# A hybrid attention and DeltaNet block on one core: one place for the matmuls' operands in memory, a tile of its own for turned q, k, v, and an earlier place for the output's first loads

## The chip, the core and the metric

The kernel runs on one core of a Trainium2 chip. The metric is device time in microseconds (us), as the median of runs; lower is better. Five instruction streams matter: PE (TensorE, matmuls and transposes), DVE (VectorE), ACT (ScalarE), POOL (GpSimd) and SP (SyncE, which here only issues DMAs). Each stream runs its instructions in the order in which they were written. PEld in a profile is the loading of a matmul's stationary operand.

## What is computed

One decoder block on x of 1024 tokens by 1024 features, fp32, from the reference, cut:

```python
h = rmsnorm(x, norm1_w)
proj = h @ w_in            # sb_q, sb_k, sb_v, sb_z, g_q, g_k, g_v, g_z, g_b, g_a
o_sb = stick_breaking_attention(sb_q, sb_k, sb_v)        # 8 heads of 64
o_sb = rmsnorm(o_sb, sb_norm_w) * silu(sb_z)
qkv = silu(causal_depthwise_conv([g_q, g_k, g_v], gdn_conv_w))   # 4 taps
o_gdn = gated_delta_chunked(l2norm(gq), l2norm(gk), gv, decay, beta)  # 4 heads of 128
o_gdn = rmsnorm(o_gdn, gdn_norm_w) * silu(g_z)
x = x + concat([o_sb, o_gdn]) @ w_out
return rmsnorm(x, final_norm_w)
```

## The kernel before

**Matmuls in three parts.** Nearly all large products run on numbers of type fp32r: an operand is split into a high part `h` (a copy rounded to fp32r by ACT) and a low part `l` (the remainder, by DVE or POOL), and `mm3` makes h·h, h·l and l·h. In a matmul the moving operand streams past (usually 512 columns) and the stationary one (128 x 128) is loaded ahead of it. In a profile's names `pp<-xl,weh` the tile ahead of the arrow is the PSUM bank; in the product of input and weights `xh`, `xl` (input) move and `weh`, `wel` (weights) are stationary.

**Stages.** First q for the attention (`wqh`, `wql`), then v and the DeltaNet's gates from the weights `chl` (eight tiles of 2 x 520 columns, in h and l: 264 columns for the first half of v, 256 for the second). Then `projections()` goes through the other columns in the fixed order ORDER, while the attention (`window`, tiles `kh`, `kl`, `q`, `ahl`, `v2a`) and the DeltaNet (`gdn_pre`, `gdn_inv`, `gdn_chain`) run between its matmuls. At the end come the output's products: first the DeltaNet's half (`products_delta`, eight blocks of 128 tokens, weights `wo`), then the attention's (`products_attention`, weights `woh`, `wol`). In these the weights move and the block's values `mmf` are stationary.

**What sets the order.** The kernel is written as streams that yield; a small planner (`Model`, `interleave`) replays them with costs of its own and fixes the order of the instructions on every engine and of the DMAs on SP. The third argument of a `Stream` is the rank of its instructions: of those that are ready the lowest goes first. Any change of a tile, a wait or a rank therefore moves instructions all over the program.

**Names that the text uses.** `g_evac` (lines 901 to 938) takes the projection of a DeltaNet q, k or v: ACT copies it into `pre` (two buffers, pool gd), DVE and ACT form the convolution in PSUM and `ac`, ACT writes the sigmoid into the same `pre`, POOL multiplies `ac` by it. For heads 2 and 3 DVE then turns `ac` in squares of 32 by 32, and four DMAs store it:

```python
sg = pre[:, 0:512]
...
first(V.transpose, sg, ac)
turned = gt_s[h, kind, ts, :].rearrange("(b r) d -> r b d", r=32)
done += [S.dma_start(turned[:, :, 32 * a:32 * a + 32], sg[32 * a:32 * a + 32, :]...) for a in range(4)]
```

So `pre` is free again only when those DMAs have read it. `k_evac` and `z_evac` use a one-buffer tile tagged `sqh` for the high part of k and for the gate's sigmoid `zs`.

`enter_delta` (line 1553) loads, for each block of the DeltaNet's half, its values (`mgf<-og_s`) and its gate (`mgf<-gate_s`); `split` multiplies them (DVE), and ACT and POOL make the parts `mmf`. `out_norm` (line 1452) loads the attention's finished outputs (`bothf<-o_s`, four DMAs a block), which ACT, DVE and POOL (`oss`) normalise for the second half.

**Places in memory.** Each tile has an address within the partition. By the program as built, taken modulo 256 bytes, moving and stationary operand of the fp32r matmuls stand so:

| matmuls (moving, stationary) | number | before: moving, stationary |
|---|---|---|
| projections `xh`/`xl`, `weh`/`wel` | 1152 | 96, 96 |
| q `xh`/`xl`, `wqh`/`wql` | 192 | 96, 96 |
| scores `kh`/`kl`, `q` | 192 | 160, 160 |
| attention's values `ahl`, `v2a` | 160 | 160, 0 or 224 |
| v and gates `chl`, `xh`/`xl` | 384 | 0 to 224, 96 |
| output, DeltaNet's half `wo`, `mmf` | 192 | 0, 32, 96, 160 or 224, 128 |
| output, attention's half `woh`/`wol`, `mmf` | 204 | 64, 128 |

So 1,576 of these have both operands at one place modulo 256, and 900 have not.

Of the kernel before, what the change touches and what calls it, by code (L numbers as in the profile page):

```python
# [10 lines left out]
F32 = mybir.dt.float32  # L11
# [6 lines left out]
P = 128  # L18
T = 1024
# [472 lines left out]
def block(tc, xT_d, x_d, n1_d, wE_d, wQ_d, wC_d, conv_d, alog_d, dtb_d, mixw_d, wo_d, fnw_d, out_d):  # L492
# [4 lines left out]
    with ExitStack() as top:  # L497
# [66 lines left out]
        xl = px.tile([P, NK, T], F32R, name="xl")  # L564
        s0_ctx = top.enter_context(ExitStack())
        s0 = open_pool("s0", ctx=s0_ctx)
        n1 = s0.tile([P, 24], F32, name="n1")[:, 0:NK]
        rbc = s0.tile([P, T], F32, name="rbc")

        def turned(tp, parts):  # L570
# [45 lines left out]
        def q_evac(pt, i, half):  # L616
            hs = slice(half * 512, (half + 1) * 512)
            j = 2 * i + half
            apart = j == 3
            if apart:  # L620
                hi, lo = [pr.tile([P, 512], F32R, tag="kt", bufs=2, name="xq") for _ in range(2)]
            else:
                t = at_.tile([P, 2, 512], F32R, tag="ahl", bufs=2, name="xq") if j in (1, 5) else s0.tile([P, 2, 512], F32R, tag="xr", bufs=5, name="xq")
# [12 lines left out]
        chl = []  # L636
        for tag, bufs in (("kh", 1), ("kl", 1), ("q2", 1), ("v2a", 1), ("sg2", 1), ("cc", 2), ("cc", 2), ("sg3", 1)):
            if tag[0] == "s":
                chl.append(fx.tile([P, 2, 520], F32R, "chl", tag))
            elif tag == "v2a":  # L640
                chl.append(Two(*[at_.tile([P, 520], F32R, tag=tag + c, name="chl") for c in "xy"]))
            else:
                t = at_.tile([P, 1040 + (48 if tag == "kl" else 0)], F32R, tag=tag, bufs=bufs, name="chl")
                chl.append(t[:, 0:1040].rearrange("p (a e) -> p a e", a=2))
# [70 lines left out]
        for b in range(NB):  # L715
            wc = s0.tile([P, 520], F32, tag="wcr", bufs=6, name="wcr")
            loads[f"c{b}"] = [S.dma_start(wc, wC_d[:, b, :])]
            A.activation(chl[b][:, 0, :], wc, AF.Copy)
            (V if b < 2 else G).tensor_tensor(chl[b][:, 1, :], wc, chl[b][:, 0, :].bitcast(F32), ALU.subtract)
        loads["s"] = [scale]  # L720
        first_loads = [op for name in LOADS for op in loads[name]]
        for a, b in zip(first_loads, first_loads[1:]):
# [39 lines left out]
        for k0 in range(0, NK, 2):  # L762
            for b in range(NB):
                bs = slice(b * P, (b + 1) * P)
                for k in (k0, k0 + 1):
                    mm3(vp[b][:, 0:264], xh[:, k, bs], xl[:, k, bs], chl[k][:, 0, 0:264], chl[k][:, 1, 0:264], k == 0, k == NK - 1)
# [30 lines left out]
        def values():  # L797
            for b in range(NB):
                yield lambda: ps.room("pp", 2)
                bs = slice(b * P, (b + 1) * P)  # L800
                pt = pp()
                for k in range(NK):
                    mm3(pt[:, 0:256], xh[:, k, bs], xl[:, k, bs], chl[k][:, 0, 264:520], chl[k][:, 1, 264:520], k == 0, k == NK - 1)
# [97 lines left out]
        def g_evac(h, kind):  # L901
            wv = conv[:, 4 * kind + h, :]
            last = []

            def evac(pt, half):
                pre = gd.tile([P, 515], F32, tag="pre", bufs=2, name="pre")
                if half == 0:
                    A.activation(pre[:, 0:3], step[:, 0:3], AF.Copy)
                else:
                    A.activation(pre[:, 0:3], last[0][:, 512:515], AF.Copy)  # L910
                last.append(pre)
                first(A.activation, pre[:, 3:515], pt, AF.Copy)
                ac = pr.tile([P, 512], F32, tag="kt", bufs=2, name="ac")

                first(A.activation, pt, pre[:, 0:512], AF.Copy, scale=wv[:, 0:1])
                for i in range(1, 4):
                    first(V.scalar_tensor_tensor, ac if i == 3 else pt, pre[:, i:i + 512], wv[:, i:i + 1], pt, ALU.mult, ALU.add)
                sg = pre[:, 0:512]
                first(A.activation, sg, ac, AF.Sigmoid)
                ts = slice(half * 512, half * 512 + 512)  # L920
                if h < TURNED and kind < 2:
                    kq = operand(h, half)
                    ck.prio, prio = BANK, ck.prio
                    r = G.tensor_tensor(kq[:, :, 1 - kind, :], ac.rearrange("p (c t) -> p c t", c=4), sg.rearrange("p (c t) -> p c t", c=4), ALU.mult)
                    ck.prio = prio
                    return r
                first(G.tensor_tensor, ac, ac, sg, ALU.mult)
                if h < TURNED:
                    return S.dma_start(g_s[h, kind, :, ts], ac)
                ck.prio, prio = STORES, ck.prio  # L930
                done = [S.dma_start(g_s[h, kind, :, ts], ac)] if kind < 2 else []
                first(V.transpose, sg, ac)
                turned = gt_s[h, kind, ts, :].rearrange("(b r) d -> r b d", r=32)
                done += [S.dma_start(turned[:, :, 32 * a:32 * a + 32], sg[32 * a:32 * a + 32, :].rearrange("r (b c) -> r b c", c=32)) for a in range(4)]
                ck.prio = prio
                return done

            return evac
# [387 lines left out]
        def attention():  # L1326
            yield lambda: "v1" in flags and "dec" in flags
            for i in range(2):
                ccs.append(at_.tile([P, T + 1], F32, tag="cc", bufs=2, name="cc"))
# [169 lines left out]
            ck.free(w)  # L1499

        def out_weights():
            places = [(t, 2 if t in ("cc", "ahl") else 1) for t in ("kh", "kl", "q2", "cc", "cc", "v2a", "ahl", "ahl")]
            for n, k in enumerate(range(4, 8)):
                yield lambda: k in raws and (n < 2 or f"e{SBH - 1}3" in flags)
                yield raws[k][1]
                weight(k, *[Two(*[at_.tile([P, 512], F32R, tag=t + c, name="wo") for c in "xy"]) if t == "v2a" else at_.tile([P, D], F32R, tag=t, bufs=m, name="wo") for t, m in places[2 * n:2 * n + 2]])
                yield

        def out_weights_attention():
            yield lambda: "g" in flags  # L1510
            gdn_ctx.close()
            f0 = pools[0] = open_pool("f0", before=gd.ops())
            flags["pool0"] = True
            for k in range(4):
                yield lambda: k in raws
# [114 lines left out]
        def products_attention():  # L1630
            yield lambda: f"d{NB - 1}" in flags
            for b in range(NB):
# [3 lines left out]
                for got in product(b, 0, parts):  # L1636
# [87 lines left out]
```

## Time and profile before

| what | value |
|---|---|
| median of 3 runs | 637.1 us (636.01 to 638.25) |
| the profiled execution | 638.77 us, its span 637.0 us |
| busy: PE, DVE, ACT, POOL | 98%, 71%, 62%, 54% of the span |
| mean granted PE clock | 0.993 |
| DMA moved | 115.99 MB, mean 182 GB/s |

The span runs from the first to the last instruction; 1.77 us of the profiled execution lie around it. The busy share of PE counts each matmul from its start to a modelled end, and successive matmuls overlap, so time that is lost between matmuls is read from their starts.

### The profile page before, as it was taken

To read this page: it belongs to the slowest core of one execution; us is meant where nothing else is said; L and a number is where in the kernel's file an instruction comes from. 1 tells how busy PE (TensorE), PEld (TensorE's weight loads), DVE (VectorE), ACT (ScalarE), POOL (GpSimd) and SP (SyncE) were. 2 spreads that over 40 slices of the span, in tenths; PEclk is the share of its full clock that TensorE was granted. 3 is DMA by queue.
4 is the path that set the end of the run, shared out by engine and by line. 5 is a ranking of instruction groups with operands and counts; after the bars stand their busy time and mean duration, and the time that the engine had idled before them with its cause. 6 is when DMAs were issued, how large, how long until landed. Compare 5 with 4: busy or idle time off the path is not lost.

```text
span 637.0 us, 11159 instructions
## 1 busy us (share of the span) xinstructions
PE 623.7 (98%) x3672; PEld 528.3 (83%) x3672; DVE 451.4 (71%) x799; ACT 396.1 (62%) x957; POOL 345.7 (54%) x429
## 2 busy tenths in 40 slices
PE   8999999999999999899999999999999998999995
PEld 7889988988888888788888888888878886887884
DVE  4469974322787896796789687677898875387774
ACT  5765578724786784776688766576868753132553
POOL 0124047828795596692697682486753426145533
PEclk9999999999999999999999999999999998999998
DMA  8968326866317428678747974525562387987642
GB/s 301 330 204 309 118 87 205 269 195 216 105 40 259 135 78 227 161 183 220 216 109 157 298 206 139 188 92 152 154 190 67 133 179 263 291 243 167 159 136 99
DMA packets 162233, 115.99 MB, mean 182 GB/s; under 512 B 95168, under 2 KB 130176, under 8 KB 162176
## 3 DMA queue, kind: packets, MB, share of 16 engines
q1 hardware_dynamic: 161888, 115.09, 60.4%
q8 instruction: 29, 0.48, 0.3%
q14 instruction: 28, 0.23, 0.1%
q10 hardware_dynamic: 288, 0.20, 0.1%
HBM read 78.12 MB, written 37.13 MB: 181 GB/s over the span
## 4 chain that ended last, share of the span: by engine, by line
PE 83%; issue 4%; DMA 4%; POOL 3%; DVE 2%; ACT 2%; SPq 1%; POOLq 0%; DVEq 0%; ACTq 0%
PE pp L376 49%; PE pz L376 23%; PE po L376 7%; PE pc L376 3%; POOL mmf L376 1%; DMA dtf<-cum_s 1%; SPq L376 1%; DMA gate_s<-zt 1%; DMA gt_s<-pre 1%; DVE cc L376 1%; DMA mgf<-og_s 0%; POOL dtf L376 0%; POOL oss L376 0%; DMA og_s<-akf 0%; DVE pp L376 0%
## 5 line engine op out<-in xcount | busy, mean ns | idle before, releaser
L376 PE MATMUL pp<-xh,weh 128*128 128x512 f32 x360 | 145.7, 405 | 0.0
L376 PE MATMUL pp<-xh,wel 128*128 128x512 f32 x360 | 141.3, 392 | 0.0
L376 PE MATMUL pp<-xl,weh 128*128 128x512 f32 x360 | 140.6, 390 | 0.0
L376 POOL TENSOR_TENSOR sgf<-sgf,cc 128x128 f32<-128x128 f32 (+3 forms) x64 | 77.1, 1208 | 48.8 <-DVE cc L376 45.1
L376 POOL TENSOR_TENSOR wel<-wer,weh 128x512 fp32r<-128x512 f32 x48 | 63.1, 1316 | 67.4 <-ACT weh L376 67.4
L376 PEld LDWEIGHTS pp<-xh,wel 128*128 128x128 f32 x360 | 67.5, 188 | 15.2
L376 PEld LDWEIGHTS pp<-xh,weh 128*128 128x128 f32 x360 | 67.7, 188 | 11.9
L376 PEld LDWEIGHTS pp<-xl,weh 128*128 128x128 f32 x360 | 67.8, 188 | 11.6
L376 DVE TENSOR_TENSOR_SCAN cc<-pz,step 128x384 f32<-128x384 f32 (+2 forms) x64 | 53.9, 847 | 8.1 <-ACT pz L376 6.7
L376 ACT ACTIVATE sgf<-pz,rs 128x384 f32<-128x384 f32 (+3 forms) x96 | 54.2, 593 | 7.4 <-PE pz L376 7.3
L376 ACT ACTIVATE ahl<-pz 128x512 fp32r<-128x512 f32 (+1 forms) x80 | 43.5, 559 | 19.9 <-PE pz L376 19.1
L376 DVE TENSOR_TENSOR ahl<-pz,ahl 128x512 fp32r<-128x512 f32 (+1 forms) x80 | 49.3, 628 | 6.5 <-ACT ahl L376 6.2
L376 ACT ACTIVATE pz<-pz,ns 128x384 f32<-128x384 f32 (+3 forms) x96 | 53.5, 575 | 0.0
L376 PE MATMUL po<-ahl,v2a 128*128 128x512 f32 (+1 forms) x160 | 49.1, 400 | 1.1 <-DVE ahl L376 1.1
L376 PE MATMUL pp<-wo,mmf 128*128 128x512 f32 x192 | 47.7, 407 | 2.2 <-POOL mmf L376 1.4
L376 PEld LDWEIGHTS pp<-wo,mmf 128*128 128x128 f32 x192 | 36.7, 194 | 12.0 <-POOL mmf L376 1.8
L376 DVE SCALAR_TENSOR_TENSOR pp<-pre,conv,pp 128x512 f32<-128x512 f32 x42 | 31.4, 747 | 20.2 <-ACT pp L376 19.7
L376 PE MATMUL pp<-woh,mmf 128*128 128x512 f32 (+2 forms) x136 | 41.8, 384 | 0.0
L376 DVE TENSOR_TENSOR_SCAN cc<-pz,cc,step 128x512 f32<-128x512 f32 (+1 forms) x32 | 38.7, 1208 | 3.6 <-ACT pz L376 3.1
L376 DVE TENSOR_TENSOR xr<-pp,xr 128x512 f32<-128x512 f32 (+2 forms) x33 | 22.1, 672 | 23.7 <-PE pp L376 23.4
L376 POOL TENSOR_TENSOR mmf<-mgf,mmf 128x512 fp32r<-128x512 f32 x16 | 21.8, 1375 | 29.0 <-ACT mmf L376 29.0
L376 PE MATMUL pz<-kh,q 128*128 128x384 f32 (+3 forms) x96 | 35.7, 377 | 0.9 <-DVE cc L376 0.9
(318 smaller groups left out, 1522.5 us busy)
## 6 DMA issues: line engine op xcount, KB each, us to landing
wer<-wE SPq DMA_DIRECT2D x48, 256.0 KB, 4.0
xr<-x SPq DMA_DIRECT2D x16, 512.0 KB, 7.0
v_s<-v2e SPq DMA_DIRECT2D x16, 256.0 KB, 2.7
v2a<-v_s SPq DMA_DIRECT2D x16, 256.0 KB, 2.9
q<-qk_s SPq DMA_DIRECT2D x8, 512.0 KB, 4.0
kh<-qk_s SPq DMA_DIRECT2D x8, 512.0 KB, 3.7
kl<-qk_s SPq DMA_DIRECT2D x8, 512.0 KB, 7.2
o_s<-oe SPq DMA_DIRECT2D x32, 128.0 KB, 3.2
```

The lines of the kernel that those rows point to most:

```text
L376: ins = f(*args, **kw).ins
```

## The change

Three things. First, tiles are resized, padded and split, so that the operands of the fp32r matmuls stand at 128 modulo 256. In the table above, all rows but one become 128, 128. In the row of `chl` the 192 matmuls of 256 columns become 128, 128, and of the 192 of 264 columns 64 do; in all 2,348 pairs are equal and 128 are not. For this each weight tile `chl` is split in two (`c1` with 264 columns, `c2` with 256), so its high part takes two ACT instructions in place of one, and its low part two of DVE or POOL. Second, the turned q, k, v go to a tile `tn` that shares the one buffer tagged `sqh`. Third, `enter_delta` gets rank OUTPUT - 4 = 8 in place of 12; `out_norm` stays at 11. The diff, cut:

```diff
-        n1 = s0.tile([P, 24], F32, name="n1")[:, 0:NK]
+        n1 = s0.tile([P, 32], F32, name="n1")[:, 0:NK]
...
-        chl = []
-        for tag, bufs in (("kh", 1), ("kl", 1), ("q2", 1), ("v2a", 1), ("sg2", 1), ("cc", 2), ("cc", 2), ("sg3", 1)):
...
+        c1, c2 = [], []
+        for tag, size, n in (("kh", 1024, 2), ("kl", 1088, 2), ("q2", 1024, 2), ("v2ax", 512, 1), ("v2ay", 512, 1), ("cc0", 1088, 2)):
+            t = at_.tile([P, size], F32R, tag=tag, name="chl")
+            width = 264 if tag == "kl" else 256
+            (c1 if tag == "kl" else c2).extend(t[:, 2 * width * m:2 * width * (m + 1)].rearrange("p (a e) -> p a e", a=2) for m in range(n))
...
-            A.activation(chl[b][:, 0, :], wc, AF.Copy)
-            (V if b < 2 else G).tensor_tensor(chl[b][:, 1, :], wc, chl[b][:, 0, :].bitcast(F32), ALU.subtract)
+            for t, w in ((c1[b], wc[:, 0:264]), (c2[b], wc[:, 264:520])):
+                A.activation(t[:, 0, :], w, AF.Copy)
+                (V if b < 2 else G).tensor_tensor(t[:, 1, :], w, t[:, 0, :].bitcast(F32), ALU.subtract)
...
                 done = [S.dma_start(g_s[h, kind, :, ts], ac)] if kind < 2 else []
+                sg = pr.tile([P, 512], F32, tag="sqh", bufs=1, name="tn")
                 first(V.transpose, sg, ac)
...
-                kh = at_.tile([P, 1040], F32R, tag="kh", name="kh")[:, 16:1040]
+                kh = at_.tile([P, T], F32R, tag="kh", name="kh")
...
+            f0.tile([P, 16], F32, name="pad")
...
-                    Stream(enter_delta(), 9.3, OUTPUT), Stream(prepare(1), 9.2, OUTPUT), Stream(products_delta(), 101, OUTPUT),
+                    Stream(enter_delta(), 9.3, OUTPUT - 4), Stream(prepare(1), 9.2, OUTPUT), Stream(products_delta(), 101, OUTPUT),
```

The matmuls and their shapes are the same ones; ACT has 8 instructions more, POOL 6 and DVE 2.

What the ranks move is seen on SP, where the output's first loads are issued (`worf` are raw output weights, `og_s<-akf` stores the DeltaNet's results). Before:

```order
L376 DMA og_s<-akf_4143 32x16x32 x4
L376 DMA worf_6457<-wo 128x1024
L376 DMA bothf_6488<-o_s 32x32x32
L376 DMA o_s<-oe 128x256
L376 DMA bothf_6488<-o_s 32x32x32 x3
L376 DMA bothf_6493<-o_s 32x32x32 x4
L376 DMA mgf_6379<-og_s 128x512
L376 DMA mgf_6379<-gate_s 128x4x128
L376 DMA mgf_6382<-og_s 128x512
```

After:

```order
L376 DMA bothf_6466<-o_s 32x32x32
L376 DMA o_s<-oe 128x256
L376 DMA bothf_6466<-o_s 32x32x32
L376 DMA mgf_6360<-og_s 128x512
L376 DMA mgf_6360<-gate_s 128x4x128
L376 DMA mgf_6363<-og_s 128x512
L376 DMA mgf_6363<-gate_s 128x4x128
L376 DMA mgf_6421<-og_s 128x512
L376 DMA mgf_6421<-gate_s 128x4x128
L376 DMA bothf_6466<-o_s 32x32x32 x2
L376 DMA bothf_6471<-o_s 32x32x32 x4
```

Six of the eight loads `bothf` now stand behind the first six loads `mgf` in place of ahead of them. On ACT, at the start of the DeltaNet's products, before:

```order
L376 ACTIVATE bothf_6488<-bothf_6488 128x8x64
L376 ACTIVATE vr<-pc,r2b 128x128
L376 ACTIVATE kqf_4572<-pz 128x128
L376 ACTIVATE pz,norms<-pz 128x128
L376 ACTIVATE bothf_6493<-bothf_6493 128x8x64
L376 ACTIVATE kqf_4572<-pz 128x128
L376 ACTIVATE pz,norms<-pz 128x128
L376 ACTIVATE mmf_6625<-mgf_6379 128x512
```

After:

```order
L376 ACTIVATE mmf_6575<-mgf_6360 128x512
L376 ACTIVATE kqf_4657<-pz 128x128
L376 ACTIVATE pz,norms<-pz 128x128
L376 ACTIVATE mmf_6600<-mgf_6363 128x512
L376 ACTIVATE mmf_6618<-mgf_6421 128x512
L376 ACTIVATE zs<-pp 128x512
L376 ACTIVATE bothf_6466<-bothf_6466 128x8x64
L376 ACTIVATE bothf_6471<-bothf_6471 128x8x64
```

The first parts `mmf` now precede both blocks `bothf` and the last step of the DeltaNet's chain (`kqf`, `norms`). On SP, where the second and third turned tiles of head 2 are stored, before:

```order
L376 DMA g_s<-ac 128x512
L376 DMA gt_s<-pre 32x16x32
L376 DMA xd_101<-xs 32x16x16 x2
L376 DMA xe<-xs 64x128
L376 DMA gt_s<-pre 32x16x32 x2
L376 DMA akf_2913<-gt_s 128x4x128
L376 DMA gt_s<-pre 32x16x32
```

After, at the same place:

```order
L376 DMA g_s<-ac 128x512
L376 DMA gt_s<-tn 32x16x32 x4
L376 DMA kh<-qk_s 128x1x1024
L376 DMA q_2852<-qk_s 128x1x1024
L376 DMA kl<-qk_s 128x1x1024
L376 DMA o_s<-oe 128x256
L376 DMA g_s<-ac 128x512
L376 DMA gt_s<-tn 32x16x32 x4
```

The four stores of a turned tile now stand together, with other transfers between one tile and the next.

More of the change, by code (lines that the diff above doesn't have):

```diff
@@ L622, in q_evac @@
             else:
-                t = at_.tile([P, 2, 512], F32R, tag="ahl", bufs=2, name="xq") if j in (1, 5) else s0.tile([P, 2, 512], F32R, tag="xr", bufs=5, name="xq")
+                t = xq1 if j == 1 else at_.tile([P, 2, 512], F32R, tag="ahl", bufs=2, name="xq") if j == 5 else s0.tile([P, 2, 512], F32R, tag="xr", bufs=5, name="xq")
                 hi, lo = t[:, 0, :], t[:, 1, :]
@@ L633, in q_evac @@
             ck.prio = prio
-        chl = []
-        for tag, bufs in (("kh", 1), ("kl", 1), ("q2", 1), ("v2a", 1), ("sg2", 1), ("cc", 2), ("cc", 2), ("sg3", 1)):
[L638 to L644, printed above, removed]
+        c1, c2 = [], []
[3 more added lines that the diff above has]
+            (c1 if tag == "kl" else c2).extend(t[:, 2 * width * m:2 * width * (m + 1)].rearrange("p (a e) -> p a e", a=2) for m in range(n))
+        for tag, n in (("sg2", 2), ("sg3", 3)):
+            t = fx.tile([P, 528 * n], F32R, "chl", tag)
+            c1.extend(t[:, 528 * m:528 * (m + 1)].rearrange("p (a e) -> p a e", a=2) for m in range(n))
+        xq1 = at_.tile([P, 2, 512], F32R, tag="ahl", bufs=2, name="xq")
+        c1.append(at_.tile([P, 528], F32R, tag="cc1", name="chl").rearrange("p (a e) -> p a e", a=2))
         sm = fx.tile([P, 768], F32, "sm", "sg1")
@@ L765, in block @@
                 for k in (k0, k0 + 1):
-                    mm3(vp[b][:, 0:264], xh[:, k, bs], xl[:, k, bs], chl[k][:, 0, 0:264], chl[k][:, 1, 0:264], k == 0, k == NK - 1)
+                    mm3(vp[b][:, 0:264], xh[:, k, bs], xl[:, k, bs], c1[k][:, 0, :], c1[k][:, 1, :], k == 0, k == NK - 1)
             for k in (k0, k0 + 1):
@@ L802, in values @@
                 for k in range(NK):
-                    mm3(pt[:, 0:256], xh[:, k, bs], xl[:, k, bs], chl[k][:, 0, 264:520], chl[k][:, 1, 264:520], k == 0, k == NK - 1)
+                    mm3(pt[:, 0:256], xh[:, k, bs], xl[:, k, bs], c2[k][:, 0, :], c2[k][:, 1, :], k == 0, k == NK - 1)
                     if k % 2 and k < NK - 1:
@@ L1328, in attention @@
             for i in range(2):
-                ccs.append(at_.tile([P, T + 1], F32, tag="cc", bufs=2, name="cc"))
+                ccs.append(at_.tile([P, T + 1], F32, tag=f"cc{i}", name="cc"))
                 V.memset(ccs[i][:, T:T + 1], 0.0)
@@ L1501, in out_weights @@
         def out_weights():
-            places = [(t, 2 if t in ("cc", "ahl") else 1) for t in ("kh", "kl", "q2", "cc", "cc", "v2a", "ahl", "ahl")]
+            places = [(t, 2 if t == "ahl" else 1) for t in ("kh", "kl", "q2", "cc0", "cc1", "v2a", "ahl", "ahl")]
             for n, k in enumerate(range(4, 8)):
```

## The prediction

> **What bounds the kernel now.** I read the page's busy times first, then the chain that ended last, then who PE waited for.
>
> ```profile
> span 637.0 us, 11159 instructions
> PE 623.7 (98%) x3672; PEld 528.3 (83%) x3672; DVE 451.4 (71%) x799; ACT 396.1 (62%) x957; POOL 345.7 (54%) x429
> PE 83%; issue 4%; DMA 4%; POOL 3%; DVE 2%; ACT 2%; SPq 1%; POOLq 0%; DVEq 0%; ACTq 0%
> ```
>
> PE is busy for 98% of the span and makes up 83% of the chain; no other engine comes near. So a matmul that starts the next one sooner is worth what it saves, almost anywhere, and work of another engine counts only where PE stands still for it. PE's waits (engine, for whom: us in total, times, longest) are few:
>
> ```profile
> PE pp L376 <- POOL mmf L376: 1.4, 1, 1.4
> PE po L376 <- DVE ahl L376: 1.1, 1, 1.1
> PE pz L376 <- DVE cc L376: 0.9, 1, 0.9
> PE pp L376 <- ACT mmf L376: 0.8, 2, 0.5
> ```
>
> The change speaks to all four: the lines with `mmf` lie at the output's first products, the other two, as shown below, behind a store of a turned tile. The rest of its bet is on the pace of the matmuls themselves.
>
> **First part: the operands' places.** The durations in the page overlap, so I take the pace from rows that merge many matmuls: start, us, how many. The first four are pieces of the chain, the other two of PE's timeline.
>
> ```profile
> 73.29 5.46 PE pp L376 x24
> 78.75 5.44 PE pz L376 x24
> 592.98 13.36 PE pp L376 x57
> 606.99 12.66 PE pp L376 x54
> 547.66 18.55 PE L376 MATMUL pp<-wo,mmf 128*128 128x512 f32 x79
> 277.19 1.89 PE L376 MATMUL pz<-kqf 128*128 128x256 f32 x8
> ```
>
> The projections, with both operands at 96, start one 512-column matmul every 5.46 / 24 = 227 ns. The output's second half, moving at 64 and stationary at 128, needs 13.36 / 57 = 234 ns; its first half, with mixed places, (18.55 - 0.39) / 78 = 233 ns, where 0.39 is the length of a single one. All have the same structure (three matmuls a pair of operands, nothing waited for), so of what I can see only the places differ. The groups that the change brings to equal places, and two that are equal already, by shape (count | busy us, mean ns of one | idle):
>
> ```profile
> L376 PE MATMUL pp<-xl,weh 128*128 128x512 f32 x360 | 140.6, 390 | 0.0
> L376 PE MATMUL pz<-kl,q 128*128 128x512 f32 x40 | 15.8, 394 | 0.0
> L376 PE MATMUL pp<-wo,mmf 128*128 128x512 f32 x192 | 47.7, 407 | 2.2 <-POOL mmf L376 1.4 <-ACT mmf L376 0.8
> L376 PE MATMUL pp<-woh,mmf 128*128 128x512 f32 x120 | 38.7, 397 | 0.0
> L376 PE MATMUL pp<-wol,mmf 128*128 128x512 f32 x60 | 23.7, 394 | 0.0
> L376 PE MATMUL po<-ahl,v2a 128*128 128x512 f32 x128 | 45.3, 430 | 1.1 <-DVE ahl L376 1.1
> L376 PE MATMUL pp<-chl,xh 128*128 128x256 f32 x96 | 18.2, 286 | 0.3 <-DVE v2e L376 0.3
> ```
>
> If equal places give 227 ns: `wo` 192 x 6 ns = 1.1 us, `woh` and `wol` 180 x 7 ns = 1.3 us, `ahl` 128 x 6 ns = 0.8 us. For `chl`, twice narrower, I take 2 ns for each of the 144 of 256 columns, 0.3 us. Together 3.5 us, all on PE's path. No row shows a 512-column matmul with both operands at 128. The ends are: 0, if the places have nothing to do with it, and 25 us. That end goes by the nearest row at 128, 128: the eight passes of `kqf`, (1.89 - 0.38) / 7 = 216 ns each (fp32, 256 columns, twice as long a column). If every 512-column fp32r matmul came to 216, the 1,424 with equal places would save 11 ns each (16 us) and the 500 others 17.5 ns (9 us). I take 3.5, since the equal pairs at 96 are the nearest in type and shape; that 128 is a better place than 96 nothing here shows.
>
> The Trainium skill, page "SBUF — State Buffer", section "Who interferes with whom", speaks against this term: PE has two independent read ports, one for the moving operand and one for the weights, and "PE and ACT never wait on anyone". By it the term is 0 and the sum 3.5 us higher, as in rival B below. The trace's 227 against 234 ns does not fit that page, unless something else in the output's stage slows PE. The page "TensorE: Matmul & The Clock Gate", section "Back-to-back issue gap", gives 512 / 2.4 + 2.5 = 216 ns, an estimate by which the projections' 227 have 11 ns to lose; whether their place is the cause it doesn't say.
>
> **Second part: the output's first loads.** PE's timeline, then SP, DVE, ACT and POOL at the start of the DeltaNet's products, then that stretch in a view by windows (clock after the busy times):
>
> ```profile
> 532.51 0.40 PE L376 MATMUL pp<-xh,wel 128*128 128x512 f32 x1
> 533.38 0.72 PE L376 MATMUL pp<-wo,mmf 128*128 128x512 f32 x2 [0.47 <-ACT mmf L376]
> 535.52 5.79 PE L376 MATMUL pp<-wo,mmf 128*128 128x512 f32 x17 [1.42 <-POOL mmf L376]
> 518.91 5.12 SPq L376 DMA_DIRECT2D bothf<-o_s  x7
> 524.08 0.76 SPq L376 DMA_DIRECT2D mgf<-og_s  x1
> 529.86 0.69 DVE L376 TENSOR_TENSOR mgf<-mgf 128x512 f32<-128x512 f32 x1
> 532.71 0.62 ACT L376 ACTIVATE mmf<-mgf 128x512 fp32r<-128x512 f32 x1
> 534.20 1.27 POOL L376 TENSOR_TENSOR mmf<-mgf,mmf 128x512 fp32r<-128x512 f32 x1
> 535.00:540.00 5.00, 4.48 (x13) 3.52 (x14) 1.27 (x2) 0.00 (x0) 5.00 (x5) 0.66 0.84 299
> ```
>
> PE's projections are over and it stands waiting for `mmf`: 533.38 - 532.51 - 0.23 = 0.64 us for ACT's part, then 535.52 - 533.38 - 2 x 0.233 - 0.1 = 1.58 us for POOL's (0.1 is how far the second row's two starts lie beyond the pace: 0.72 - 0.39 = 0.33 us between them). The clock answers: in the stretch of 5 us behind it is 0.66, and the 17 matmuls take (5.79 - 0.39) / 16 = 0.338 us each in place of 0.233, 16 x 0.105 = 1.68 us. Together 3.9 us. The reason is in the order: `mgf` is loaded only at 524.08, directly behind seven loads `bothf` of 5.12 / 7 = 0.73 us each, and DVE, ACT and POOL follow one another. In the changed order six loads `bothf` stand behind six `mgf`, so the first `mgf` is issued 6 x 0.73 = 4.4 us sooner (ends: 0 and 5.1), more than the 2.2 us that PE stood; ACT and POOL, whose queues had `bothf` and the DeltaNet's last step ahead, take `mmf` first. So I take the whole 3.9. The gain lies between 0 (the products wait for DVE or the last `og_s` instead) and 3.9. Below nothing it can go through what is late next: the attention's blocks `bothf` come six transfers, some 4.4 us, later (rival E), and the DeltaNet's last `kqf` stands on ACT behind an `mmf` of 0.62 us, which delays only the blocks that come last.
>
> **Third part: the tile `tn`.** The chain, ACT's, PE's and DVE's timeline, and DVE's group:
>
> ```profile
> 250.40 4.81 DMA gt_s<-pre
> 255.29 0.20 ACT L376 ACTIVATE pre<-pre 128x3 f32<-128x3 f32 x1 [5.28 <-DMA gt_s<-pre]
> 258.04 0.62 PE L376 MATMUL po<-ahl,v2a 128*128 128x512 f32 x2 [1.11 <-DVE ahl L376]
> 260.68 0.39 PE L376 MATMUL pz<-kh,q 128*128 128x256 f32 x1 [0.91 <-DVE cc L376]
> 248.35 0.71 DVE L376 STREAM_TRANSPOSE pre<-ac 128x512 f32<-128x512 f32 x1 [0.32 <-POOL ac L376]
> L376 DVE STREAM_TRANSPOSE pre<-ac 128x512 f32<-128x512 f32 x12 | 8.4, 704 | 2.4 <-POOL ac L376 1.6 <-DMA wer<-wE 0.7
> ```
>
> ACT stands 5.28 us for a store that reads `pre`, and just behind it PE stands for DVE's `ahl` and `cc`, which need ACT's results: 1.11 + 0.91 = 2.02 us by the rows. With `tn` ACT's next `pre` no longer needs that store, so those 2.0 us go, unless DVE is late there anyway. It is the only such wait that PE felt: the other tiles of the twelve cost it nothing. Against it: `tn` has one buffer, shared with `k_evac` and `z_evac`, where turned tiles had two. DVE's next transpose, or ACT's `zs`, must now wait for all four stores of the tile before. At this place the next transpose (248.35) would have stood until 250.40 + 4.81 = 255.2, 6.9 us. But the planner knows the wait and puts the four stores of a tile together, and DVE has 29% of its time free. Ends: -2.0 us, and +2.0 for each transpose that stands as long as ACT did. I take -2.0 (rival D is the other end).
>
> **Fourth part: more instructions, another order.** ACT's parts of `chl`, POOL's last work on them, and PE's chain at the last two weight tiles:
>
> ```profile
> L376 ACT ACTIVATE chl<-wcr 128x520 fp32r<-128x520 f32 x6 | 3.7, 639 | 0.2 <-DMA wcr<-wC 0.2
> 54.87 2.29 POOL L376 TENSOR_TENSOR chlf<-wcr,chlf 128x520 fp32r<-128x520 f32 x1
> 67.46 1.46 PE pp L376 x12
> ```
>
> Two halves for one of 0.639 us cost an instruction's fixed part more; the shortest ACT row here is 0.20 us (255.29), so 8 x 0.20 = 1.6 us on ACT, and as much on POOL and DVE. The last low part is ready at 54.87 + 2.29 = 57.2, PE takes the last weights at 67.46: 10 us of cover. I take 0 (ends 0 and 1.6). If that cover is gone, PE waits for the tile then at the head, at most those 1.6 us.
>
> And every instruction between is placed anew by the planner. PE's order changes all over, and a stall like the ones above can come up or go anywhere. The four rows of waits bound it: none of them costs PE over 2.2 us. I take +1.5, most of one such stall; ends 0 and two of 2.2.
>
> **Sum.** -3.5 - 3.9 - 2.0 + 0 + 1.5 = -7.9 us against the profiled execution of 638.8, which lies 1.7 above the median of 637.1. On the median: 629.2, said as 629 us. About 0.3%, 1.9 us, is what a measurement of this kernel can tell from no change.
>
> **The rivals.**
> B: the places do nothing. For it speaks that in the output's half other things than places differ too (weights move, DMAs run); against it that `woh`, with nothing waited for, stays at 234 over 57 matmuls in a row. 629.2 + 3.5 = 632.7.
> C: 128 is a better place than 96. For it speaks `kqf` at 216 ns; against it that `kqf` is fp32, whose columns take twice as long to stream, and that `kl,q` (both at 160) has the mean of the projections (394 and 390), so that the common place seems not to matter. Between 227 and 216 ns a matmul: 629 - 21 = 608 to 624.
> E: the places do nothing and the gain at 533 is given back at the attention's half. The chain there:
>
> ```profile
> 572.36 2.62 POOL oss L376
> 577.05 3.71 PE pp L376 x15
> ```
>
> POOL's `oss` stands in the chain just ahead of PE's next products, so `out_norm` has little slack at 577; `bothf` comes 4.4 us later, and PE would stand as long as it did at 533. It decides if DVE, ACT and POOL cannot make up those 4.4 us in the 40 us between. 632.7 + 3.9 = 636.6, no change.
> D, slower: the single buffer of `tn`. A transpose that waits for four stores holds up DVE, and with it `ahl` and `cc`, on which PE stood 2.0 us behind the one long wait shown. Five such stalls eat the forecast's gain of 7.9 and the 2.0; with all eleven followers late it is 629 + 2 + 22 = 653, with six 643. Against it: DVE's transposes have waited 2.4 us in all, and only the one store at 250 took 4.81.
>
> The places themselves follow from the program, so that the change does nothing at all is no rival.
>
> **How the numbers follow.** Forecast (629, own range 625 to 633) 0.45; B (633) 0.14; C (608 to 624) 0.19; E (637) 0.12; D (639 to 653) 0.10. The range of 610 to 638 leaves out D and the far end of C, about 0.15. Faster by over 0.3%: forecast, B, C, 0.78; the same: E, 0.12; slower: D, 0.10.
>
> **What the next profile would show.** Places: pieces of the chain in the output's stage at 227 ns a matmul, and `wo`, `woh`, `wol`, `ahl` by shape with means near 390 while `xl,weh` stays there; if `xl,weh` drops below 380 it is C, if `woh` stays near 397 B. Loads: no PE wait on `mmf`, and a clock of 1.0 where it was 0.66; a new wait on `mmf` behind `oss` is E. `tn`: no ACT wait of 5 us on a store, and DVE's transposes with little idle time on DMA `gt_s`; some us there and PE waits on `ahl` or `cc` are D. It would be wrong if PE's summed waits grew by over 5 us at a place that no step names, or if matmuls of equal place ran at two paces.

## The result, and the profile after

The changed kernel takes 630.48 us (median of 6 runs, 628.49 to 632.6), the kernel before 637.26 us beside it (6 runs, 635.26 to 638.25): a ratio of 0.9904, 95% interval 0.9883 to 0.9924, or 6.8 us less. The forecast was 629 us, with a range of 610 to 638. The profiled execution took 631.83 us against 638.77, 6.9 us less, so the two traces can be set against each other as they are. First the lines of the page on the span, the busy times and the chain of the changed kernel:

```profile
span 630.1 us, 11144 instructions
PE 618.9 (98%) x3672; PEld 526.6 (84%) x3672; DVE 448.7 (71%) x801; ACT 395.8 (63%) x965; POOL 346.5 (55%) x435
PE 83%; DMA 5%; DVE 4%; SPq 3%; issue 2%; ACT 2%; POOL 1%; POOLq 0%; DVEq 0%; ACTq 0%
```

PE still bounds the kernel, with the same shares; its busy time fell by 4.8 us. Its waits (engine, for whom: us in total, times, longest) are now these:

```profile
PE po L376 <- DVE step L376: 1.7, 1, 1.7
PE pp L376 <- DVE xr L376: 1.5, 2, 1.4
PE pz L376 <- DVE cc L376: 0.3, 1, 0.3
```

The first one, for `step`, is the start of the program and stood there before. The waits for `mmf`, `ahl` and `cc` of 0.8 to 1.4 us are gone. New is 1.5 us for `xr`, the tile to which DVE adds the output's products. The groups by shape (count | busy us, mean ns of one | idle) that the change brought to equal places, and one that was there already:

```profile
L376 PE MATMUL pp<-xl,weh 128*128 128x512 f32 x360 | 140.7, 391 | 0.0
L376 PE MATMUL pp<-wo,mmf 128*128 128x512 f32 x192 | 45.0, 392 | 1.5 <-DVE xr L376 1.5
L376 PE MATMUL pp<-woh,mmf 128*128 128x512 f32 x120 | 38.3, 394 | 0.0
L376 PE MATMUL pp<-wol,mmf 128*128 128x512 f32 x60 | 23.4, 389 | 0.0
L376 PE MATMUL po<-ahl,v2a 128*128 128x512 f32 x128 | 45.6, 431 | 0.0
```

`wo` went from 407 to 392 ns, `woh` from 397 to 394 and `wol` from 394 to 389. `xl,weh`, whose two operands went from 96 to 128 together, stays where it was (390, 391), and `ahl` doesn't move (430, 431).

The durations overlap, so the sums were made from the starts in the two traces: the time from each matmul's start to the next one's, added up by product (us).

| product | before | after | difference |
|---|---|---|---|
| output, DeltaNet's half `wo` (192) | 48.80 | 45.78 | -3.0 |
| output, attention's half `woh`, `wol` (204; the last has no next start) | 45.23 | 44.36 | -0.9 |
| projections (1152) | 270.69 | 268.89 | -1.8 |
| scores `kh`, `kl` (192) | 39.41 | 38.69 | -0.7 |
| v and gates `chl` (384) | 47.13 | 46.65 | -0.5 |
| attention's values `ahl` (160) | 38.21 | 38.61 | +0.4 |
| all others, q among them | 138.68 | 138.21 | -0.5 |
| first to last start | 628.15 | 621.19 | -7.0 |

The place where the output's products begin, in PE's timeline and in a view by windows (behind the busy times the clock, the DMA share and GB/s):

```profile
529.65 0.39 PE L376 MATMUL pp<-xh,wel 128*128 128x512 f32 x1
529.87 10.36 PE L376 MATMUL pp<-wo,mmf 128*128 128x512 f32 x45
```

```profile
535.00:540.00 5.00, 5.00 (x24) 4.14 (x23) 1.38 (x2) 0.63 (x1) 1.29 (x1) 1.00 0.61 176
```

PE goes from the last projection to the first product in 529.87 - 529.65 = 0.22 us and runs 45 matmuls at (10.36 - 0.39) / 44 = 227 ns, where it had stood 2.2 us and then run 17 at the clock of 0.66. The clock is now 1.00.

### The profile page after: what moved, and what is told of

Read it like the earlier page. It is cut to its first block, busy times and chain, and to the rows that moved or that the text cites. A ratio compares the mean times of both kernels' runs of the same rounds, so it can differ in the third digit from the quotient of the medians.

```text
span 630.1 us, 11144 instructions
## 1 busy us (share of the span) xinstructions
PE 618.9 (98%) x3672; PEld 526.6 (84%) x3672; DVE 448.7 (71%) x801; ACT 395.8 (63%) x965; POOL 346.5 (55%) x435
## 4 chain that ended last, share of the span: by engine, by line
PE 83%; DMA 5%; DVE 4%; SPq 3%; issue 2%; ACT 2%; POOL 1%; POOLq 0%; DVEq 0%; ACTq 0%
PE pp L376 49%; PE pz L376 24%; PE po L376 6%; PE pc L376 3%; SPq L376 3%; DVE cc L376 1%; DMA kl<-qk_s 1%; DMA xr<-x 1%; DMA xr1f<-xT 1%; DMA og_s<-akf 1%; DMA bothf<-o_s 1%; ACT sgf L376 1%; DVE pp L376 0%; DVE ahl L376 0%; ACT pz L376 0%
## 5 line engine op out<-in xcount | busy, mean ns | idle before, releaser
L376 ACT ACTIVATE pz<-pz,ns 128x384 f32<-128x384 f32 (+3 forms) x96 | 52.2, 572 | 0.0
L376 PE MATMUL pp<-wo,mmf 128*128 128x512 f32 x192 | 45.0, 392 | 1.5 <-DVE xr L376 1.5
L376 PEld LDWEIGHTS pz<-step,stf 128*128 128x128 f32 x288 | 30.8, 141 | 5.2
```

What stands on the lines that cost most here:

```text
L376: ins = f(*args, **kw).ins
```

## The experiments

**The three parts alone, and two by two.** Each kernel is one of the three parts, or two, on the kernel before. The edits are pieces of the diff above: "rank" is the one number of `enter_delta`, "tn" is the one line that makes `tn`, "places" is all the rest (with the split weights `chl`). The first three:

```diff
p1_places: all of the change but these two
-                sg = pr.tile([P, 512], F32, tag="sqh", bufs=1, name="tn")
-                    Stream(enter_delta(), 9.3, OUTPUT - 4), ...
+                    Stream(enter_delta(), 9.3, OUTPUT), ...
t1_turned: the kernel before, and
+                sg = pr.tile([P, 512], F32, tag="sqh", bufs=1, name="tn")
r1_rank: the kernel before, and
-                    Stream(enter_delta(), 9.3, OUTPUT), ...
+                    Stream(enter_delta(), 9.3, OUTPUT - 4), ...
```

Places alone, expected:

> The places alone (turned tiles stay in `pre`, the output's first loads keep rank 12). If equal places are what quickens the output's products: `wo`, `woh` and `wol` start one matmul per 227 ns as in the changed kernel, against 233 before, about 372 x 5.5 ns = 2.0 us less, ahl and chl little; PE's waits for `mmf` near 532 (2.2 us, with the clock's dip 3.9) and behind the store near 255 (2.4 us) remain unless the new order moves them: 635 us, between 633 and 637. Rival: the pace in the output's stage comes from the other two parts (fewer waits, another clock): 233 ns stays and the time is that of before, 637. If the new order itself brings what the changed kernel gained at no named place (about 1 us fewer changes of kind and no wait near 113 us), this kernel shows it too, since its order differs from before's from the first weights on.

The tile `tn` alone, expected:

> The tile `tn` alone, on the kernel before: all places, and the output's rank, as before. Theory: ACT's wait of 5.3 us for a store near 250 goes, and with it PE's two stalls of 2.4 us start to start; DVE's transposes wait a few us in all for the one buffer: 634.5 to 635.5, and the clock's dip near 533 stays. Rival D: the one buffer holds up DVE, PE waits for ahl or cc at other places, 637 or more. Rival: ACT's wait had nothing to do with PE's stalls: the wait goes, PE's stalls near 258 and 261 stay, 637.

The rank alone, expected:

> The rank of the output's first loads alone, on the kernel before: places and turned tiles as before. Theory: PE's waits for `mmf` near 532 and the dip of the clock behind them go (3.9 us), and part of it, about 1.5 us, comes back near 565 to 570 as a wait of PE for DVE's `xr`, because DVE stands for the later loads `bothf`: 634 to 635.5. Rival: the wait near 565 in the changed kernel belongs to the faster products of that kernel (places), not to the rank: no such wait here, 633. Rival E of the prediction: all comes back, 637.

After these came the pairs. `a_notn` is the changed kernel without the line of `tn`, `a_norank` the changed kernel with the rank of before, `a_noplace` the kernel before with the line of `tn` and the new rank. Places and rank, expected:

> Places and rank, without `tn`: the changed kernel with turned tiles put back into `pre`. If `tn` is worth the 2.4 us of the wait near 255 here, 633. If `tn` costs as much as alone (5.6 us), 625. If that wait was an accident of one order, which another order of the same instructions doesn't have (with the places alone DVE's and ACT's waits for those stores were gone too), `tn` is worth nothing here: 630 to 632, with no wait of ACT for a store.

Places and `tn`, expected:

> Places and `tn`, without the rank: the changed kernel with the output's first loads at rank 12 again. If the rank is worth what it is alone (1.9 us), 632.5. If the 3.9 us at `mmf` come back, less the 1.5 us at `xr` that go, 633. If `tn` costs 5.6 us also beside the places, 641; the changed kernel's DVE didn't wait for a store of `tn`, so that is not expected.

Rank and `tn`, expected:

> Rank and `tn`, without the places: the kernel before with these two alone. If the three parts added up, 637 - 1.9 + 6.3 = 641. If `tn` costs only where DVE's transposes meet unfinished stores of the tile before (4.5 us of DVE's time in the kernel with `tn` alone), this kernel shows those waits and PE's stalls near 250 to 390 too, since the rank acts only behind 490: 640 to 641. If the cost was an accident of one order, 634 to 637.

All seven, against the kernel before on the same chip (its medians lay between 636.7 and 637.3):

| kernel | median us | ratio (95% interval) |
|---|---|---|
| places | 635.37 | 0.9965 (0.9938 to 0.9991) |
| tn | 643.00 | 1.0087 (1.0064 to 1.0109) |
| rank | 634.79 | 0.9975 (0.9958 to 0.9993) |
| places, rank | 636.24 | 0.9988 (0.9971 to 1.0006) |
| places, tn | 631.30 | 0.9914 (0.9894 to 0.9933) |
| tn, rank | 643.12 | 1.0100 (1.0079 to 1.0120) |
| all three | 630.48 | 0.9904 (0.9883 to 0.9924) |

None of the three pairs came out at a time that I had named: 636.24 for 625 to 633, 631.30 for 632.5 to 641, 643.12 for 634 to 641. The parts do not add up. `tn` costs 6 to 8 us without the places, and beside places and rank it gains: 636.24 without it, 630.48 with it, intervals apart. The rank gains 1.9 us alone, and beside any other part it moves the time by less than the intervals. Places alone gain 1.3 us by the medians, places with `tn` 5.4.

The median of the places alone hides something. Of its twelve executions the four with a granted clock of 0.997 or more took 630.43 to 632.98 us, the eight with 0.996 or less 634.34 to 638.38. The profiled one is among the four: from first to last start it needs 622.2 us, 1.0 more than the changed kernel. So a good part of what separates the two medians is in executions of which there is no trace.

In the kernel with `tn` alone, the waits that rival D named are in plain sight. DVE's transposes by group (behind the second bar the idle time ahead of them):

```profile
L376 DVE STREAM_TRANSPOSE tn<-ac 128x512 f32<-128x512 f32 x12 | 8.5, 705 | 6.6 <-DMA gt_s<-tn 4.5 <-POOL ac L376 1.8 <-DMA og_s<-akf 0.2
```

DVE's and SP's timeline at one tile of that kernel:

```profile
240.99 0.71 DVE L376 STREAM_TRANSPOSE tn<-ac 128x512 f32<-128x512 f32 x1
244.55 0.38 SPq L376 DMA_DIRECT2D gt_s<-tn  x1
245.02 1.48 SPq L376 DMA_DIRECT2D xd<-xs  x2
247.22 1.11 SPq L376 DMA_DIRECT2D gt_s<-tn  x2
248.94 0.52 SPq L376 DMA_DIRECT2D gt_s<-tn  x1
253.24 0.71 DVE L376 STREAM_TRANSPOSE tn<-ac 128x512 f32<-128x512 f32 x1 [3.27 <-DMA gt_s<-tn]
```

The tile is turned at 241.0, its last store is issued at 248.9, and the next transpose, on the one buffer, stands 3.27 us for it. In the changed kernel the same group reads:

```profile
L376 DVE STREAM_TRANSPOSE tn<-ac 128x512 f32<-128x512 f32 x12 | 8.3, 695 | 0.0
```

No transpose waits there. The places alone show the same for `pre` (idle 0.0), and ACT has no wait for a store either: the wait of 5.28 us, for which `tn` was to be a cure, is absent in that kernel without `tn`.

The rank alone, PE's timeline at the output's start:

```profile
530.35 5.75 PE L376 MATMUL pp<-wo,mmf 128*128 128x512 f32 x24
537.93 4.46 PE L376 MATMUL pp<-wo,mmf 128*128 128x512 f32 x18 [1.82 <-DVE xr L376]
```

The waits for `mmf` go, as expected, and one of 1.82 us for `xr` comes 8 us later, not near 565 as I had expected. But the stall isn't bound to the rank. With places and `tn` and the old rank, SP and PE stand so:

```profile
508.70 7.62 SPq L376 DMA_DIRECT2D bothf<-o_s  x7
516.37 0.69 SPq L376 DMA_DIRECT2D mgf<-og_s  x1
529.30 0.39 PE L376 MATMUL pp<-xh,wel 128*128 128x512 f32 x1
529.53 15.80 PE L376 MATMUL pp<-wo,mmf 128*128 128x512 f32 x69
```

The seven `bothf` are still ahead of `mgf`, and PE doesn't stand: here `mgf` is issued 529.53 - 516.37 = 13.2 us ahead of the first product, in the kernel before 533.38 - 524.08 = 9.3 us. (PE's waits have no line with `mmf` in the kernels with the places alone and with `tn` alone either.) With the places alone the lead is 12.5 us, and PE doesn't stand either. What `mgf` needs is a lead, and a place ahead of `bothf` is one way to it.

**Places, in an order that doesn't change.** These two kernels have the changed kernel's instructions in its order, on every engine; only addresses differ. In the first, pads move the eight weight tiles of the attention's half:

```diff
-                weight(k, *[f0.tile([P, D], F32R, name=f"wo{c}{k}") for c in "hl"])
+                both_ = []
+                for c in "hl":
+                    if k or c == "l":
+                        f0.tile([P, 8], F32, name=f"pad{c}{k}")
+                    both_.append(f0.tile([P, D], F32R, name=f"wo{c}{k}"))
+                weight(k, *both_)
```

> The changed kernel with eight small pads between the eight weight tiles of the attention's half, so that these (moving) stand at 128, 160, 192, 224, 0, 32, 64 and 96 modulo 256 while the stationary `mmf` stays at 128; the instructions and their order are the same. Theory: the pair at 128, 128 starts one 512-column matmul per 227 ns, every other 230 to 235, about 140 x 5.5 ns = 0.8 us more time in all. If only the place modulo 64 counts, 0, 64 and 192 are at 227 too; if modulo 128, 0 is. Rival (the places do nothing): all eight at 227. If one of them lies near 216, a better place than the common one exists.

From the starts in its trace, for 512 columns moving with `mmf` at 128 (ns to the next start, mean of those without a stall; 206 at 128, 15 or 28 at each other place):

| moving at, modulo 256 | 128 | 64 | 192 | 160 | 0 | 32 | 96 | 224 |
|---|---|---|---|---|---|---|---|---|
| ns | 228.1 | 229.7 | 229.9 | 231.4 | 231.5 | 232.9 | 234.4 | 234.9 |

The attention's half took 45.00 us in place of 44.36, 0.64 more (0.8 expected). So unequal places cost, but the single columns say less than they seem to. Most of the 206 at 128 are `wo`, in the half that was not swept; the 28 in the swept half, which stand among matmuls at 64, 160 and 192, have a mean of 231.2 ns, where the same matmuls had 228.8 in the changed kernel. And 64, here 229.7, gave 233.2 ns in the kernel before, where all of that half stands there. A matmul's interval therefore depends on its neighbours' places too. That equality modulo 64 is not enough follows from the kernel before; whether modulo 128 is, stays open. No place comes near 216. The single time of 632.33 us says nothing by itself.

The second moves the projected input by 32 bytes, so that all projections and q stand at 96 and 128 (and the stationary operand of `chl` at 96):

```diff
         xl = px.tile([P, NK, T], F32R, name="xl")
+        px.tile([P, 8], F32, name="shift")
```

> The changed kernel with a pad of 32 bytes behind the projected input, so that `xh` and `xl` stand at 96 modulo 256 and the weights stay at 128; instructions and order are the same ones. Theory (equal places matter, by what the sweep showed for 96 against 128, 234.4 against 227.6 ns): 1,344 matmuls of 512 columns in the projections and q take 6.8 ns more each, 9.1 us in all: 639 to 640, with `xl,weh` at 234 ns start to start. Rival (the pace depends on the stage, the places matter only in the output): 630.5, as the changed kernel.

It took 635.63 us, 0.9984 (0.9966 to 1.0002) of the kernel before, against the changed kernel's 0.9904: nearly the whole gain is spent, 5.1 us by the medians. The chain of the changed kernel and of this one, at the same matmuls of the projections:

```profile
73.01 5.44 PE pp L376 x24
78.45 5.44 PE pz L376 x24
```

```profile
74.34 5.60 PE pp L376 x24
79.95 5.60 PE pz L376 x24
```

5.44 / 24 = 227 ns against 5.60 / 24 = 233 ns. Over all projections the mean of regular starts went from 228.8 to 233.0 ns. The size was 4 to 6 ns and not the expected 6.8; the projections' starts add up to 4.6 us more and q's to 1.1. From first to last start the trace is only 2.9 us longer, in part because the wait of 1.36 us for `xr` is not in it, although the order is the changed kernel's. That places act is shown for matmuls of 512 columns, in the projections, in q and in the output. The 256-column matmuls of `chl` did not pay for it: they start every 116.7 ns here, 119.8 in the changed kernel, where their places are equal, and 118.4 in the kernel before.

**What `tn` alone pays for.** If late stores on one buffer were the price, putting the four stores first on SP should bring the time back:

```diff
+                ck.prio = OUT_WEIGHTS
                 done += [S.dma_start(turned[:, :, 32 * a:32 * a + 32], ...) for a in range(4)]
```

> The kernel with `tn` alone, its four stores of a tile raised ahead of everything else on SP, so that they stand together behind each transpose. Theory: `tn` alone cost 6.3 us because its stores were issued 4 to 8 us late between other transfers and the next transpose stood on DVE for them (3.3 and 1.2 us); then DVE's waits for those stores go and the time is 636 to 639. Rival: the waits go and PE's stalls stay, since it is the order of the attention's and the DeltaNet's steps that costs: 642 or more.

It took 652.08 us, 1.0235 (1.0202 to 1.0269). The stores stand together behind each transpose and DVE waits only 1.7 us for them, but PE's waits are led by two that had not been there:

```profile
PE pz L376 <- DVE cc L376: 5.5, 2, 5.0
PE pz L376 <- issue: 3.0, 1, 3.0
```

So my theory of `tn`'s price fell: less of the named wait, and 9 us more time. Two more kernels ask what merely another order is worth. Both change one cost of the planner; one is on the kernel with `tn` alone, one on the kernel before:

```diff
-HOPS = {"A": 145, "G": 75, "P": 197, "V": 130, "S": 900}
+HOPS = {"A": 145, "G": 75, "P": 197, "V": 135, "S": 900}
```

> The kernel with `tn` alone, with one cost of the planner changed from 130 to 135 ns (a hop from DVE to another engine), which moves some 500 of DVE's rows. If the 6.3 us belong to the shared single buffer, they stay: 642 to 644. If they belong to one order, the time is anywhere between 634 and 644.

> The kernel before with the same cost of the planner changed from 130 to 135 ns, which moves some 430 of DVE's rows and nothing else. It shows what a new order alone is worth: if between -1 and +1 us, the sums of parts can be taken at their word; if it moves the time by 3 us or more, no part of this change under that size can be told from its order.

With `tn` alone 639.14 us, 1.0041 (1.0026 to 1.0057), 3.9 us better than 643.00 by 5 ns in one number. And its transposes wait as long as they did:

```profile
L376 DVE STREAM_TRANSPOSE tn<-ac 128x512 f32<-128x512 f32 x12 | 8.4, 704 | 6.6 <-DMA gt_s<-tn 4.7 <-POOL ac L376 1.8
```

The kernel before: 636.11 us, 0.9989 (0.9971 to 1.0007), no difference, though PE's stall at the output's start shrank and others came up. So the order alone was worth 0 once and 4 us once, and the wait of DVE doesn't set the price.

What sets it shows in PE's rows and in a view by windows (the clock behind the busy times). First `tn` alone, then `tn` alone with the 5 ns:

```profile
377.90 1.70 PE L376 MATMUL pz<-wc,dt 32*32 32x32 f32 x32 [2.48 <-DVE dt L376]
378.00:388.00 10.00, 10.00 (x99) 8.59 (x99) 6.58 (x11) 2.22 (x6) 3.22 (x3) 0.50 0.88 290
```

```profile
305.73 0.80 PE L376 MATMUL pp<-xh,weh 128*128 128x512 f32 x1 [1.55 <-DVE kt L376]
305.30:308.60 3.30, 2.87 (x7) 2.31 (x8) 2.55 (x5) 2.27 (x5) 1.92 (x2) 0.50 0.62 216
```

With the end of a wait of PE the granted clock goes to half, for 10.24 us in the first and for 3.41 us in the second; 512-column matmuls then start every 427 ns in place of 227. I estimate the cost at half of each stretch: 5.1 and 1.7 us. The waits themselves differ little (those over 0.25 us, from 10 us on, add up to 5.9 and 5.5 us). The kernel before has 3.41 us at half clock too, behind its waits for `mmf`. So the clock accounts for 3.4 us, by this estimate, of the 3.6 that `tn` alone is longer in its trace from first to last start (631.76 and 628.15). With `tn` and rank 6.83 us are at half clock, with the stores in front 13.65, and the traces of the kernels with the places have no such stretch before PE's work ends. The executions without a trace agree: the mean granted clock was 0.989 to 0.992 in all six with `tn` alone, 0.994 to 0.998 with the 5 ns. The wait of 2.48 us itself is not behind a late store: the last transpose ahead of it, at 370.83, stood for nothing, and DVE waited for nothing from there to `dt`.

**One number of the planner, for the new wait.** In the changed kernel PE's 1.36 us wait at 567.66 has this ahead of it on DVE:

```profile
565.65 0.69 DVE L376 TENSOR_TENSOR bothf<-bothf 128x512 f32<-128x512 f32 x1 [1.69 <-DMA bothf<-o_s]
566.26 0.68 DVE L376 TENSOR_TENSOR mgf<-pz,mgf 128x512 f32<-128x512 f32 x1
566.93 0.68 DVE L376 TENSOR_TENSOR xr<-pp,xr 128x512 f32<-128x512 f32 x1
567.66 3.01 PE L376 MATMUL pp<-wo,mmf 128*128 128x512 f32 x12 [1.36 <-DVE xr L376]
```

DVE stands 1.69 us for a late `bothf`, and `xr`, which frees PE's bank, is queued behind it. The planner counts 475 ns of SP for each such load. The 0.7 to 1.25 us of the expectation below are not the rule: the 32 loads of the changed kernel's trace have a median of 0.56 us, and the longest took 4.46.

```diff
-            cost = 475
+            slow = op.prio == OUTPUT - 1
+            cost = 900 if slow else 475
...
-            self.at(self.dma + 1500, self.finish, op)
+            self.at(self.dma + (3000 if slow else 1500), self.finish, op)
```

> The changed kernel, with one number of the planner corrected: the loads `bothf` are planned at 900 ns of SP each and land 3000 ns later, in place of 475 and 1500, since the profile shows 0.7 to 1.25 us for each on SP. Theory: DVE's `bothf` then stands behind `xr` where its load is late, so PE's waits for `xr` near 564 (1.5 us) go: 629. Rival: another wait comes up in the new order: 630.5 or more.

The wait is not there; PE's list has only the program's start and two of 0.3 us:

```profile
PE po L377 <- DVE step L377: 1.7, 1, 1.7
PE pz L377 <- DVE cc L377: 0.3, 1, 0.3
PE pz L377 <- ACT wy L377: 0.3, 1, 0.3
```

The time is 630.60 us, 0.9904 (0.9881 to 0.9928): as the changed kernel's. Its profiled execution (628.86) was the fastest of its six, the changed kernel's (631.83) one of the slower; the 1.5 us are within what runs of one kernel differ by, 628.86 to 632.76 here. The version is no worse, and not shown to be better. Nor is it shown that the edit removed the wait: in the changed kernel's own order the shifted kernel has no wait for `xr` either, and the swept one has 0.7 us in two.

## Why the prediction was right, and where its steps were not

The time was right, 630.5 for 629. The sum came out, but two of its causes were wrong.

**Places: 3.5 us forecast, 2.0 measured.** By starts, `wo` went from 232.7 to 227.4 ns (192 x 5.3 = 1.0 us) and the 512-column part of `woh` and `wol` from 233.2 to 227.9 (180 x 5.3 = 1.0 us); forecast 1.1 and 1.3. `ahl` gave 233 to 232 ns on those of its matmuls that run undisturbed, under 0.1 us for the forecast 0.8: of the intervals from one `ahl` to the next, 53 of 92 before and 58 of 91 after are longer than 260 ns, with medians of 316 and 314, whatever the place (what holds those up was not looked into). `chl` stayed at 120.0 and 120.5 ns. The step that failed is the carrying over of the 6 ns from long rows of one kind to short rows, and of a third of it to matmuls half as wide. Rival B is excluded by the kernel with the shifted input (5.1 us in an unchanged order), rival C by `xl,weh` at 391. The sentence of the Trainium skill, page "SBUF — State Buffer", section "Who interferes with whom", that "PE and ACT never wait on anyone" does not fit the two operands of one matmul stream: 227 against 233 ns in the same order. Which accesses collide, no run shows. The 216 ns of the Trainium skill, page "TensorE: Matmul & The Clock Gate", section "Back-to-back issue gap", weren't reached at any place. That section gives them for an isolated matmul, and about 131 ns for a sustained stream of 512 columns, which is further off still; why these matmuls take 227 stays open.

**First loads: 3.9 us forecast and gone, 1.9 come back, and not for the reason given.** Of the time lost in `wo`, the two waits and the stretch at a lower clock are gone as forecast; the first `mgf` is issued 529.87 - 509.65 = 20.2 us ahead of the first product, where 9.3 + 4.4 were forecast (`wo` has 3.0 less in the table: 1.0 and 3.9 less, 1.9 more). 1.5 us came back at 567 as a wait for `xr` behind a late `bothf`, and some 0.4 in small breaks up to 574.5: rival E's mechanism at DVE in place of POOL, with half its price, in this execution. But the rank isn't what took the stall away. Without it, places and `tn` have no stall either, and 631.3 us. The failed step is "the reason is in the order", `bothf` ahead of `mgf`. It was a reason only in the kernel before, where `mgf` had 9.3 us of lead; with 12.5 and 13.2 us behind the same loads PE did not stand.

**The tile `tn`: 2.0 us forecast, and they went, also without `tn`.** PE's two waits behind ACT's 5.28 us are gone (2.4 us start to start). With the places alone they are gone too. By itself `tn` is 6.3 us slower. That is rival D's time and not its path: DVE's waits for the stores are there (4.5 us), but PE's waits grew by only 1.3 us (4.6 to 5.9), and more than that is the clock at half behind one wait of 2.48 us that no store caused. The step that failed is the price of a stall. The third and fourth part took each at its length, some 2 us, although the second part had counted the clock behind one at 1.7 us more; here 2.5 us of waiting cost 5 more. Beside the places `tn` gains 4.1 us, beside places and rank 5.8; of the latter, 3.2 us are in the projections' starts (272.04 to 268.89 from the kernel without `tn` to the changed one), with one wait of 1.7 us for `kt` and ten breaks in the stream of matmuls fewer. Why the two together give so good an order is not settled. What is shown is that 5 ns in a planner's cost are worth 3.9 us to `tn` alone, most of it by a shorter time at half clock.

**More instructions, another order: 0 and +1.5 forecast.** The split of `chl` costs nothing that shows: its sum fell by 0.5, a wait of that size near 114 having gone. For the order: 7.0 us from first to last start, less 2.0, 3.9 and 2.4, leaves +1.3, of which the new losses near 567, `xr` above all, are 1.9. The size was right, which is luck in part, since the waits near 567 come and go between executions of one order; that this term, and not the three others, decides which parts work, I had not seen. An allowance of 1.5 us with ends at 0 and 4.4 was too narrow for it: by the medians the same line `tn` went from -5.8 to +8.3 us with what stood around it, and its stores in front cost 9 more.

## What to carry to other kernels

Where a planner or scheduler orders all engines, a part's worth is that of the order it lands in: measure the parts in the combination that will stay, and check a place or a size with pads that leave every instruction where it was. A named wait that goes with a change is no proof that the change took it away; look whether it is there without the change in the neighbouring orders, and in another execution of the same order. Read the granted clock behind every wait of PE before you price it. Give the two operands of a dense stream of 512-column fp32r matmuls one place modulo 256 bytes: here 4 to 6 ns of 230, one matmul after another.

## What the runs showed of the hardware

- In a dense stream of 512-column fp32r matmuls, moving and stationary operand at one place modulo 256 bytes throughout gave a start every 227 to 229 ns (at 96 and at 128 alike), unequal places 230 to 235. With the order of instructions unchanged, 32 bytes of padding moved the projections from 228.8 to 233.0 ns and cost 5.1 us. Which distance is worst isn't settled: 64 apart gave 233.2 ns in one kernel and 229.7 in another. `chl`, of 256 columns, did not gain from equal places (118.4 ns before, 119.8 after).
- No group of these matmuls had a mean below some 227 ns at full granted clock, at any of the eight places; the eight passes of `kqf` (fp32, 256 columns) start every 216 ns.
- Between 10 us and the end of PE's work the granted clock was 1.00 or 0.50 in these traces, and 0.50 for stretches of 3.41, 6.83 or 10.24 us. All four waits of PE of 2.48 us and more had such a stretch behind them (2.48 us twice, 2.97 and 5.02). Of the shorter ones, 1.42, 1.55 and 1.85 us had one, and others of 1.55, 1.71 and 1.82 us had none. The view by windows of the kernel with the rank alone, right behind its wait of 1.82 us:

```profile
538.00:543.00 5.00, 5.00 (x22) 4.05 (x23) 1.16 (x2) 0.00 (x0) 0.84 (x1) 1.00 0.94 288
```

The clock is 1.00 there. So a wait costs its length, or two to three times that, and these cases don't show what decides below 2.5 us.
